# Weight sums of a two-level product moved from accumulating transfers to VectorE additions

## Chip, core and metric

One core of one Trainium2 chip runs the whole kernel. The metric is the device time of one execution in microseconds; the median of three executions is compared. Engines are called TensorE (PE in the rows, PEld its weight loads), VectorE (DVE), ScalarE (ACT), GpSimd (POOL) and SyncE (SP, which only issues transfers).

## The reference, cut to what matters

One decoder layer: a normalised input `h` (1024 prompt tokens and 8 decode tokens, 2048 wide) goes through one wide projection `h @ w_in`, whose columns feed sparse attention with a top-256 indexer, an mLSTM, and gates; the gated outputs go through `w_out` and a final norm.

```python
h = rmsnorm(x, norm_w)
p = split(h @ w_in)                    # q, k, v, indexer, gates, mLSTM q/k/v
att = sparse_attend(p.q, top256(indexer_scores(p.qi, p.ki, p.wi)), p.k, p.v)
ml = mlstm_run(p.mq, p.mk, p.mv, p.ig, p.lf)
x = x + concat(att * silu(p.az), norm(ml) * sigmoid(p.mo) * silu(p.mz)) @ w_out
y = rmsnorm(x, final_norm_w)
```

All of it is float32. The kernel splits each operand of a matmul into a rounded part H and a rest L and sums three products (H H, H L, L H).

## The kernel before, in words

`w_in` is worked through in 61 tiles of 128 columns. Tiles 0 to 20 (misc, indexer queries, attention k, v, q) are plain products in `proj`. Tiles 21 to 60 are the gate stage, `gate_stage`: the tokens are halved, the input rows are halved and the 40 column tiles are taken as 20 pairs (`NP`), so that seven products of half size take the place of eight (a Strassen-like scheme). The seven kinds are called 0 to 7 by the weight operand: kinds 4 to 7 are blocks b11, b12, b21, b22 of the weights as they lie in memory; kinds 1, 2 and 3 are sums of blocks, which have to be made (kind 0, b11 + b12, is only a step on the way to kind 1, which adds b22). Kind 3 is b22 + b12, kind 2 is kind 1 + b21. The order of products is kinds 4 and 6 in turn (20 pairs), then 20 of kind 1, 20 of kind 3, 20 of kind 2, and at last kinds 5 and 7.

The sums are made by transfers. `job_usum` (line 1463) issues for each sum a copy of one block into the DRAM buffer `usD` (from SP, line 1472, or POOL, line 1474) and then, on POOL, a transfer that adds another block to it (`accum_op`, line 1478). A step of the generator is one transfer, a round is four. Within a round, an addition follows the copy that it needs.

`job_usum` and other side work (gates, indexer with top-k search, decode scoring, decode selection `job_dsel`, decode attention, prompt attention, mLSTM) are generators. Three `Lane`s step through their jobs beside the main matmuls: `Lane.step` is called with the time counted in quarter tiles, and each job has a start tile, an end tile and a weight; the steps are spread evenly until the end. Before the change the third lane has "early sums" (64 steps, tile 11.5 to 22) and "late sums" (96 steps, to tile 46). If a product asks for a sum that isn't there, `wget` (line 1708) drives the lane until it is. All engine and transfer queues are in order, and their order is fixed when the kernel is built, by priorities (`tc.high_priority`), ties (`pin`) and a simulated timeline.

A product takes its weights by `wide` (line 1755): a load of 512 KB (or two of 256 KB) into a raw buffer, a cast to H on ScalarE (line 1770) and a subtraction for L on VectorE (line 1771). The ring of raw buffers has one member at first and three from the fourth load on; each member is a pair of 128x512 tiles. Two of the three are loaded whole, the third in two transfers. H and L have three buffers.

Results of a kind are put together with those of the kinds before: `get` (line 1798) loads an intermediate from `spD` into a buffer of the ring `outs`, `combine` (line 1874, its operations are at line 1877) adds PSUM to it on VectorE, `put` (line 1804) stores it. `outs` has four buffers; two more (`ones`, the halves of `rstd`) join it only in the last stage. After the gate stage, `out_weight` (line 1971) splits the first three weight blocks of the output projection; its cast and subtraction are tied into program order.

The lines 1013 and 1035 are the loads of cached indexer keys (`kp`, indirect, on POOL) and their matmuls; 1069 and 1073 are the count and its matmul in `job_dsel`.

Of the kernel before, what the change touches and what calls it, by code (L numbers as in the profile page):

```python
# [8 lines left out]
F32 = mybir.dt.float32  # L9
# [4 lines left out]
OP = mybir.AluOpType  # L14
# [28 lines left out]
T_AK = 9  # L43
T_AV = 11
T_AQ = 13
T_G = 21
# [10 lines left out]
NP = (NT - T_G) // 2  # L57
# [120 lines left out]
def body(tc, A, stop=None):  # L178
    nc = tc.nc
    V, SC, G, PE, SY = nc.vector, nc.scalar, nc.gpsimd, nc.tensor, nc.sync  # L180
# [43 lines left out]
    def paced(name, x):  # L224
        pace[name] = x.ins
        return x

    def dt_(shape, name):
        return tc.dram_tile(shape, F32, name=name)
# [12 lines left out]
    rcS = [dt_([4, S], f"rcS{j}") for j in range(2)]  # L242
    gateS = dt_([2048, R], "gateS")
    xsD = dt_([5, 8, 128, HR], "xsD")
    usD = dt_([4, NP, 128, 2, 4, 128], "usD")
    spD = dt_([3, NP, 128, HR], "spD")
    biasS = [tc.dram_tile([128, (i + 1) * 128], BF16, name=f"biasS{i}") for i in range(8)]

# [801 lines left out]
    def job_dsel():  # L1050
        NP1 = NPG + 1
        with tc.tile_pool(name="dq", bufs=1, side="right") as pd:
# [34 lines left out]
            for bit in (30,) + tuple(range(28, -1, -2)):  # L1087
                n = 1 if bit == 30 else 3
                for y in range(n):
                    v = V.tensor_scalar(cand[:, y], Tt, (y + 1) << bit, None, OP.bitwise_or)  # L1090
                    if not y:
                        pin(v)
                g3 = pd.tile([128, 3, NB, NP1], BF16, name="ri")
                V.tensor_tensor(g3[:, :n], sp.unsqueeze(1).to_broadcast([128, n, NB, NP1]),
                                cand[:, :n].bitcast(F32).unsqueeze(3).to_broadcast([128, n, NB, NP1]), OP.is_ge)
                count(g3[:, :n].rearrange("p y b g -> p (y b) g"), n)
                yield 1400 if n == 1 else 2800
                c = total(n).rearrange("p (y b) -> p y b", y=n)
                yield 300 if n == 1 else 600
                V.tensor_tensor(flag[:, :n], c, kp.unsqueeze(1).to_broadcast([128, n, NB]), OP.is_ge)  # L1100
                for y in range(n):
                    V.copy_predicated(Tt, flag[:, y], cand[:, y])
# [355 lines left out]
                yield 1  # L1458

    sums = set()  # L1460
    NE = 64

    def job_usum():
        def parts(i):
            c1 = T_G + 2 * i - 1
            return [[A["wa"][c, y] for y in range(2)] for c in (c1, c1 + 1)]

        def copy(n, i, src, queue):
            with tc.high_priority():
                if queue is SY:  # L1470
                    with tc.issue_after(pace["dma"]):
                        SY.dma_start(usD[n, i], src)
                else:
                    pin(queue.dma_start(usD[n, i], src))

        def plus(n, i, src):
            with tc.high_priority():
                pin(G.dma_start(usD[n, i], src, accum_op=OP.add, max_dma_last_dim=8192))  # L1478
            sums.add((n, i))

        for i in range(NP + 1):
            (b11, _), (b12, _) = parts(min(i, NP - 1))
            b22 = parts(i - 1)[1][1] if i else None
            if i < NP:
                copy(0, i, b11, SY)
                yield 1
            if i:
                copy(1, i - 1, usD[0, i - 1], G)
                yield 1
            if i < NP:  # L1490
                plus(0, i, b12)
                yield 1
            if i:
                plus(1, i - 1, b22)
                yield 1
        for n, src in ((3, None), (2, 1)):
            for i in range(NP):
                (_, b21), (b12, b22) = parts(i)
                copy(n, i, b22 if n == 3 else usD[1, i], SY if n == 3 else G)
                yield 1  # L1500
                plus(n, i, b12 if n == 3 else b21)
                yield 1

    def att_free():
# [18 lines left out]

    groups = ((2, 3), (4, 5), (6, 7))

    def shares(gen, n):
        g = gen()

        def part(n):
            for _ in range(n):  # L1530
                w = next(g, 0)
                if not w:
                    return
                yield w
        return lambda: part(n), lambda: part(10 ** 6)

    sums_a, sums_b = shares(job_usum, NE)
    lanes = [Lane([Job("gates", 5, T_AK - 0.5, 12500, job_gates),
                   Job("index", T_AK + 1.5, 31.5, 6000 + sum(map(ix_weight, groups)), lambda: job_index(groups)),
                   Job("att", T_G + 17.6, 49.3, 2 * 2 * sum(2 * (1 + (i + 1) * 0.5) for i in range(8)) + 18, job_att, att_free),  # L1540
# [4 lines left out]
                   Job("qrows", T_G + 0.2, 27, 1, job_qrows),  # L1545
                   Job("datt", T_G + 9.2, 38.4, 10000 + 8 * 7000 + 34000 + 5 * 2500 + 8000 + 8000 + 5000, job_datt),
                   Job("dml", T_G + 20, 55.5, 28000 + 16 * 2500 + 5000, job_dml, hi_done)]),
             Lane([Job("early sums", T_AK + 2.5, 22.0, NE, sums_a),
                   Job("late sums", T_AK, 46.0, 8 * NP - NE, sums_b)])]
    gateV = gateS.rearrange("(k p) r -> k p r", p=128)  # L1550
    mixb = [None] * KT
    first = []
# [129 lines left out]
    def gate_stage():  # L1682
# [17 lines left out]
        def take(name, ring):  # L1700
            x = ring[turn[name] % len(ring)]
            turn[name] += 1
            return x
# [2 lines left out]
            return take("ev", outs)  # L1706

        def wget(kind, i):
            if kind < 4:
                while (kind, i) not in sums:  # L1710
                    assert lanes[2]._next() is not None
                return usD[kind, i].rearrange("p q a b -> p q (a b)")
            y, x = divmod(kind - 4, 2)
            return A["wa"][T_G + 2 * i + x - 1, y].rearrange("p q a b -> p q (a b)")
# [40 lines left out]
        def wide(kind, i):  # L1755
            turn["n"] += 1
            if turn["n"] == 4:
                H, L = (wst.plain(name) for name in ("wH", "wL"))
                mlc["bc"] = raws[0][:2]
                raws[:] = [[x[:, 0], x[:, 1], x[:, 0:2]] for x in (H, L)] + [[H[:, 2], L[:, 2], None]]  # L1760
                turn["raw"] = 0
            with tc.high_priority():
                raw = take("raw", raws)
                H, L = (x[turn["w"] % 3] for x in halves)
                turn["w"] += 1
                whole = raw[2] is not None
                for q in (slice(0, 2),) if whole else range(2):
                    r = raw[2] if whole else raw[q]
                    paced("dma", SY.dma_start(r, wget(kind, i)[:, q]))
                    paced("act", SC.copy(H[:, q], r))  # L1770
                    paced("dve", V.tensor_tensor(L[:, q], r, H[:, q].bitcast(F32), OP.subtract))
            return H, L
# [130 lines left out]
                mlc["lo"] = True  # L1903
        del extra, both
        ones += [rstd[:, c * HR:c * HR + HR].rearrange("p (c t) -> p c t", c=2) for c in range(2)]
        turn["p"] = 0

        def two():
            return [take("p", pj), take("p", pj)]
# [29 lines left out]
        def flush():  # L1939
            while muls:  # L1940
                times, ks = muls.pop(0)
                times()
                ready.extend((state["u"], k) for k in ks)
# [27 lines left out]
        def out_weight(q):  # L1971
            H, L, load, cast = wload(A["wo"][0, q], 128, wst, 2, 3)
            pin(load(slice(0, 4)))
            for x in cast(slice(0, 4)):
                pin(x)
            first.append((H, L))

        def last():
# [1 line left out]
            out_weight(2)  # L1980

        flush()
        for p in range(3):
            fetch(p)
        for p, (z, i, y) in enumerate(order):
# [480 lines left out]
```

## Time and profile before

| | us |
|---|---|
| median of three executions (1964.26 to 1969.11) | 1965.51 |
| the profiled execution | 1964.0 |
| its span, first to last instruction | 1962.2 |
| TensorE busy | 1895.3 |
| VectorE busy | 1406.0 |
| ScalarE busy | 914.1 |
| POOL busy | 533.7 |

The profile shows one execution; its mean granted TensorE clock is 0.987 of full speed (2.4 GHz, the other level is 1.2). Busy times of engines overlap. Idle time before an instruction is put down to the wait that ended last; where several waits follow one another (a matmul waits for VectorE, VectorE for ScalarE, ScalarE for a load), the chain has to be followed through the rows of each engine.

### The profile page before, as it was taken

To read this page: it belongs to the slowest core of one execution; us is meant where nothing else is said; L and a number is where in the kernel's file an instruction comes from. 1 tells how busy PE (TensorE), PEld (TensorE's weight loads), DVE (VectorE), ACT (ScalarE), POOL (GpSimd) and SP (SyncE) were. 2 spreads that over 40 slices of the span, in tenths; PEclk is the share of its full clock that TensorE was granted. 3 is DMA by queue.
4 is the path that set the end of the run, shared out by engine and by line. 5 is a ranking of instruction groups with operands and counts; after the bars stand their busy time and mean duration, and the time that the engine had idled before them with its cause. 6 is when DMAs were issued, how large, how long until landed. Compare 5 with 4: busy or idle time off the path is not lost. (4 is left out here: it accounts for less than half of the span.)

```text
span 1962.2 us, 37412 instructions
## 1 busy us (share of the span) xinstructions
PE 1895.3 (97%) x13422; PEld 1820.9 (93%) x13422; DVE 1406.0 (72%) x3261; ACT 914.1 (47%) x1826; POOL 533.7 (27%) x614
## 2 busy tenths in 40 slices
PE   9999998999989999998899999999999989999997
PEld 9999998999979999998799999999999989977776
DVE  8554664767789985897465566657979866787797
ACT  8222252334543557621245565454656634454645
POOL 0599853321100001035111000001211340107632
PEclk9999998999989999999999999999999999999999
DMA  7577767879878759979998874458988778898866
GB/s 258 158 233 217 236 203 223 246 210 228 242 227 246 197 166 270 339 244 266 310 304 239 243 214 143 133 177 294 328 286 294 222 192 269 273 339 300 277 200 220
DMA packets 252918, 474.46 MB, mean 242 GB/s; under 512 B 40549, under 2 KB 116133, under 8 KB 246333
## 3 DMA queue, kind: packets, MB, share of 16 engines
q1 hardware_dynamic: 217261, 356.70, 55.8%
q0 software_dynamic: 21504, 107.32, 21.9%
q10 hardware_dynamic: 13968, 8.06, 1.4%
q8 instruction: 105, 1.72, 0.4%
q14 instruction: 80, 0.66, 0.1%
HBM read 381.54 MB, written 174.32 MB: 283 GB/s over the span
## 5 line engine op out<-in xcount | busy, mean ns | idle before, releaser
L1782 PE MATMUL pj<-xH 128*128 128x258 f32 x1920 | 548.2, 286 | 21.4 <-DVE ev L1877 14.1
L1782 PE MATMUL pj<-xL,xH 128*128 128x258 f32 x1920 | 548.2, 286 | 0.0
L1782 PE MATMUL pj<-xH,xL 128*128 128x258 f32 x1920 | 547.2, 286 | 0.0
L1782 PEld LDWEIGHTS pj<-xH 128*128 128x128 f32 x1920 | 365.2, 190 | 25.3 <-DVE ev L1877 15.3
L1782 PEld LDWEIGHTS pj<-xL,xH 128*128 128x128 f32 x1920 | 365.6, 190 | 2.4 <-issue 0.8
L1782 PEld LDWEIGHTS pj<-xH,xL 128*128 128x128 f32 x1920 | 365.4, 191 | 1.7
L1599 PE MATMUL pj<-xH,wH 128*128 128x344 f32 (+1 forms) x816 | 265.0, 328 | 1.9 <-DVE ev L385 1.1
L1599 PE MATMUL pj<-xL,wH 128*128 128x344 f32 (+1 forms) x816 | 266.2, 326 | 0.0
L1599 PE MATMUL pj<-xH,wL 128*128 128x344 f32 (+1 forms) x816 | 265.4, 326 | 0.0
L263 DVE TENSOR_TENSOR wL<-wraw,wH 128x512 fp32r<-128x512 f32 (+2 forms) x151 | 117.4, 789 | 106.2 <-ACT wH L262 99.9
L1478 POOL DMA_DIRECT2D usD<-in_wa_dram x80 | 66.5, 863 | 428.4 <-DMA usD<-in_wa_dram 228.8
L262 ACT CAST wH<-wraw 128x512 fp32r<-128x512 f32 (+2 forms) x151 | 89.8, 607 | 199.9 <-PE pj L1599 98.3
L1599 PEld LDWEIGHTS pj<-xH,wH 128*128 128x128 f32 x816 | 153.9, 189 | 3.6 <-DVE ev L385 1.8
L1599 PEld LDWEIGHTS pj<-xL,wH 128*128 128x128 f32 x816 | 154.1, 189 | 0.6 <-DVE xL L320 0.3
L1599 PEld LDWEIGHTS pj<-xH,wL 128*128 128x128 f32 x816 | 154.2, 189 | 0.4 <-DVE wL L263 0.3
L1770 ACT CAST xH<-wL 128x1024 fp32r<-128x1024 f32 (+1 forms) x91 | 76.1, 836 | 125.5 <-PE pj L1782 69.8
L1770 ACT CAST xH<-wH 128x1024 fp32r<-128x1024 f32 x91 | 76.0, 836 | 124.4 <-PE pj L1782 72.9
L2153 PE MATMUL pj<-wH,sH 128*128 128x512 f32 x336 | 131.3, 391 | 1.7 <-ACT wH L2137 1.7
L2153 PE MATMUL pj<-wH,sL 128*128 128x512 f32 x336 | 130.7, 390 | 0.0
L2153 PE MATMUL pj<-wL,sH 128*128 128x512 f32 x336 | 125.9, 393 | 4.8 <-DVE wL L2142 4.8
L477 ACT ACTIVATE rl<-bank 128x512 f32<-128x512 f32 (+2 forms) x160 | 79.8, 523 | 99.7 <-PE bank L475 55.1
L480 DVE SCALAR_TENSOR_TENSOR s<-rl,wiN,s 128x512 f32<-128x512 f32 (+2 forms) x150 | 106.6, 729 | 19.5 <-ACT rl L477 16.6
(492 smaller groups left out, 4507.4 us busy)
## 6 DMA issues: line engine op xcount, KB each, us to landing
usD<-in_wa_dram POOLq DMA_DIRECT2D x80, 512.0 KB, 7.8
wraw<-in_wt_dram SPq DMA_DIRECT2D x144, 256.0 KB
usD<-in_wa_dram SPq DMA_DIRECT2D x40, 512.0 KB
usD<-usD POOLq DMA_DIRECT2D x40, 512.0 KB, 7.2
wraw<-in_wa_dram SPq DMA_DIRECT2D x78, 256.0 KB
wraw<-in_wo_dram SPq DMA_DIRECT2D x64, 256.0 KB
ev<-spD SPq DMA_DIRECT2D x62, 258.0 KB
spD<-ev SPq DMA_DIRECT2D x60, 258.0 KB
```

Source lines behind the costliest of these rows:

```text
L262: a = SC.copy(H[:, s, :cols], raw[:, s, :cols])
L263: return a, V.tensor_tensor(L[:, s, :cols], raw[:, s, :cols], H[:, s, :cols].bitcast(F32), OP.subtract)
L477: SC.activation(r[:, :cn], p[:, :cn], AF.Relu)
L480: v = V.scalar_tensor_tensor(s[:, c0:c0 + cn], r[:, :cn], wv, s[:, c0:c0 + cn], OP.mult, OP.add)
L1478: pin(G.dma_start(usD[n, i], src, accum_op=OP.add, max_dma_last_dim=8192))
L1599: m = PE.matmul(ps[:cols, :cn], w_[:, k, :cols], x_[kk][:, c0:c0 + cn], start=(kk == ends[0] and z == 0), stop=(kk == ends[1] and z == 2))
L1770: paced("act", SC.copy(H[:, q], r))
L1782: PE.matmul(ps[c], w_[:, q, ks], x[y][:, c * CS:c * CS + CS], start=(first and q == 0 and k == 0 and z == 0), stop=(q == 1 and k == 3 and ...
L2153: PE.matmul(ps[b], S_[x][:, b * 128:b * 128 + 128], T_[y], start=(k == 0 and z == 0), stop=(k == 7 and z == 2))
```

## The change

Kinds 2 and 3 are no longer made by transfers. `wide` loads both operands of such a sum in halves (kind 2: the sum of kind 1 and b21; kind 3: b22 and b12) into the two tiles of a raw buffer, adds them on VectorE, and casts and subtracts as before; a product of these kinds takes two raw buffers in turn. `usD` has two kinds instead of four, and one job "sums" of 80 steps stands from tile 11.5 to 30.5. In a round, the POOL copy for kind 1 is two rounds behind the SP copy for kind 0, and each addition is one round behind its copy. `job_dsel` issues no step while its lane is between T_G (21) and T_G + 1.2 tiles, and 200 units of its weight move from after the count's matmul to before it. The two buffers of `ones` join `outs` from kind 1 on and leave it before the last stage, to join again at its fifth product as before. The cast and subtraction of `out_weight` are no longer tied, but get priority behind the last weight split.

```diff
-    usD = dt_([4, NP, 128, 2, 4, 128], "usD")
+    usD = dt_([2, NP, 128, 2, 4, 128], "usD")
...
                 count(g3[:, :n].rearrange("p y b g -> p (y b) g"), n)
-                yield 1400 if n == 1 else 2800
+                while T_G <= lanes[1].now / 4 < T_G + 1.2:
+                    yield None
+                yield 1600 if n == 1 else 3200
                 c = total(n).rearrange("p (y b) -> p y b", y=n)
-                yield 300 if n == 1 else 600
+                yield 100 if n == 1 else 200
...
-        for i in range(NP + 1):
-            (b11, _), (b12, _) = parts(min(i, NP - 1))
-            b22 = parts(i - 1)[1][1] if i else None
+        for i in range(NP + 3):
             if i < NP:
-                copy(0, i, b11, SY)
+                copy(0, i, parts(i)[0][0], SY)
                 yield 1
-            if i:
-                copy(1, i - 1, usD[0, i - 1], G)
+            if 2 <= i < NP + 2:
+                copy(1, i - 2, usD[0, i - 2], G)
                 yield 1
-            if i < NP:
-                plus(0, i, b12)
+            if 1 <= i <= NP:
+                plus(0, i - 1, parts(i - 1)[1][0])
                 yield 1
-            if i:
-                plus(1, i - 1, b22)
-                yield 1
-        for n, src in ((3, None), (2, 1)):
-            for i in range(NP):
-                (_, b21), (b12, b22) = parts(i)
-                copy(n, i, b22 if n == 3 else usD[1, i], SY if n == 3 else G)
-                yield 1
-                plus(n, i, b12 if n == 3 else b21)
+            if i >= 3:
+                plus(1, i - 3, parts(i - 3)[1][1])
                 yield 1
...
-             Lane([Job("early sums", T_AK + 2.5, 22.0, NE, sums_a),
-                   Job("late sums", T_AK, 46.0, 8 * NP - NE, sums_b)])]
+             Lane([Job("sums", T_AK + 2.5, 30.5, 4 * NP, job_usum)])]
...
-            if kind < 4:
+            if kind < 2:
                 while (kind, i) not in sums:
...
                 turn["w"] += 1
+                if kind in (2, 3):
+                    pair = (wget(1, i), wget(6, i)) if kind == 2 else (wget(7, i), wget(5, i))
+                    for q in range(2):
+                        raw = raw if not q else take("raw", raws)
+                        for r, src in zip(raw, pair):
+                            paced("dma", SY.dma_start(r, src[:, q]))
+                        V.tensor_tensor(raw[0], raw[0], raw[1], OP.add)
+                        paced("act", SC.copy(H[:, q], raw[0]))
+                        paced("dve", V.tensor_tensor(L[:, q], raw[0], H[:, q].bitcast(F32), OP.subtract))
+                    return H, L
...
         ones += [rstd[:, c * HR:c * HR + HR].rearrange("p (c t) -> p c t", c=2) for c in range(2)]
+        outs += ones
         turn["p"] = 0
+        turn["ev"] = 4
...
             pin(load(slice(0, 4)))
-            for x in cast(slice(0, 4)):
-                pin(x)
+            with tc.high_priority(), tc.issue_after(pace["act"]), tc.issue_after(pace["dve"]):
+                cast(slice(0, 4))
...
         flush()
+        del outs[4:]
         for p in range(3):
             fetch(p)
```

## Rows read from the trace of the kernel before

**Rows 1.** The page, part 1: busy time of each engine, its share of the span, instructions.
```profile
PE 1895.3 (97%) x13422; PEld 1820.9 (93%) x13422; DVE 1406.0 (72%) x3261; ACT 914.1 (47%) x1826; POOL 533.7 (27%) x614
```

**Rows 2.** Stretches: start:end length, busy PE, PEld, DVE, ACT, POOL, granted clock, transfer share, GB/s.
```profile
307.38:314.86 7.48, 0.00 (x1) 0.01 (x1) 0.00 (x0) 0.43 (x1) 3.68 (x5) 0.71 1.04 313
314.86:320.70 5.84, 5.84 (x24) 5.84 (x25) 0.79 (x3) 0.19 (x1) 1.06 (x1) 0.50 1.05 331
531.38:533.61 2.23, 0.00 (x1) 0.03 (x1) 2.23 (x6) 0.45 (x1) 0.03 (x1) 1.00 0.86 314
542.59:547.74 5.15, 0.00 (x1) 0.03 (x1) 4.29 (x19) 2.39 (x5) 1.29 (x2) 0.83 1.01 348
547.74:552.80 5.06, 5.06 (x23) 5.06 (x24) 2.98 (x9) 1.03 (x2) 0.79 (x1) 0.50 1.08 295
553.14:557.13 3.99, 0.00 (x1) 0.01 (x2) 3.95 (x17) 1.03 (x2) 0.52 (x1) 0.89 1.26 353
557.13:563.05 5.92, 5.59 (x26) 5.40 (x26) 5.18 (x21) 2.60 (x5) 0.00 (x0) 0.50 0.07 27
927.24:931.69 4.45, 4.45 (x20) 4.45 (x21) 3.47 (x5) 1.14 (x2) 3.42 (x4) 0.50 0.80 180
945.34:948.76 3.42, 3.42 (x17) 3.42 (x18) 1.06 (x6) 0.79 (x3) 0.34 (x1) 0.50 0.87 346
1608.00:1626.00 18.00, 12.43 (x70) 11.36 (x70) 13.68 (x28) 7.32 (x15) 3.24 (x6) 0.81 0.79 245
```

**Rows 3.** Waits of TensorE, 800 to 990 us: total, times, longest.
```profile
PE pj L1782 <- DVE ev L1877: 14.1, 6, 4.6
```

**Rows 4.** POOL's timeline, 304 to 315 us: start, length, operation, idle time before.
```profile
305.40 0.87 POOL L1478 DMA_DIRECT2D usD<-in_wa_dram  x1 [10.72 <-DMA usD<-usD]
306.57 1.06 POOL L1013 DMA_INDIRECT kp<-in_cik_dram,idx  x1 [0.31 <-issue]
```

**Rows 5.** Timelines of ScalarE and TensorE, start of the gate stage.
```profile
529.71 1.05 ACT L1770 CAST xH<-wraw 128x1024 fp32r<-128x1024 f32 x1 [6.03 <-DMA wraw<-in_wa_dram]
...
557.13 0.20 PE L1073 MATMUL bank<-cb,onesb 128*128 128x24 bf16 x1 [3.99 <-DVE cb L1069]
```

**Rows 6.** A stretch, as in rows 2: 600 to 700 us.
```profile
600.00:700.00 100.00, 100.00 (x750) 95.61 (x749) 90.40 (x187) 46.47 (x80) 5.96 (x8) 1.00 0.75 198
```

**Rows 7.** Waits of SP's queue, 800 to 985 us: total, times, longest.
```profile
SPq L1801 <- DMA spD<-ev: 80.5, 21, 9.1
```

**Rows 8.** Timelines of SP, ScalarE and VectorE, 916 to 927 us.
```profile
916.55 0.37 SPq L1769 DMA_DIRECT2D wL<-usD  x1
...
922.21 1.05 ACT L1770 CAST xH<-wL 128x1024 fp32r<-128x1024 f32 x1 [12.00 <-DMA wL<-usD]
...
926.77 0.42 DVE L1877 TENSOR_TENSOR ev<-pj,ev 128x258 f32<-128x258 f32 x1
```

**Rows 9.** Instructions that write usD, 615 to 1110 us: durations ns, first and last start.
```profile
L1478 POOL DMA_DIRECT2D usD<-in_wa_dram x40: 772/782/1432, 622.8 to 1101.2; - x40
...
L1474 POOL DMA_DIRECT2D usD<-usD x20: 556/758/777, 920.2 to 1092.5; - x20
```

**Rows 10.** Stretches, as in rows 2: the products of kinds 3 and 2.
```profile
920.00:1124.00 204.00, 187.01 (x1459) 180.03 (x1459) 114.97 (x283) 86.21 (x182) 32.31 (x47) 0.97 0.93 275
1124.00:1315.00 191.00, 191.00 (x1535) 187.41 (x1535) 117.81 (x326) 102.76 (x240) 0.00 (x0) 1.00 0.53 159
```

**Rows 11.** Timelines of ScalarE and VectorE, 1600 to 1612 us.
```profile
1604.21 1.12 ACT L262 CAST wH<-wraw 128x512 fp32r<-128x512 f32 x2
...
1608.76 0.69 DVE L263 TENSOR_TENSOR wL<-wraw,wH 128x512 fp32r<-128x512 f32 x1
```

**Rows 12.** Line 2162, an addition on VectorE: durations ns, first and last start, shape.
```profile
L2162 DVE TENSOR_TENSOR yt<-yt,x x21: 677/680/1650, 1871.8 to 1939.6; 128x512 f32<-128x512 f32 x21
```

**Rows 13.** Waits of VectorE, 800 to 990 us: total, times, longest.
```profile
DVE xL L1771 <- ACT xH L1770: 25.9, 12, 7.5
DVE ev L1877 <- DMA ev<-spD: 11.3, 3, 5.7
```

More of the change, by code (lines that the diff above doesn't have):

```diff
@@ L1460, in body, with parts @@
     sums = set()
-    NE = 64
+    def parts(i):
+        c1 = T_G + 2 * i - 1
+        return [[A["wa"][c, y] for y in range(2)] for c in (c1, c1 + 1)]
     def job_usum():
-        def parts(i):
-            c1 = T_G + 2 * i - 1
-            return [[A["wa"][c, y] for y in range(2)] for c in (c1, c1 + 1)]
         def copy(n, i, src, queue):
@@ L1524, in body @@
     groups = ((2, 3), (4, 5), (6, 7))
[L1526 to L1537, printed above, removed]
     lanes = [Lane([Job("gates", 5, T_AK - 0.5, 12500, job_gates),
```

## The prediction

> **What bounds the kernel now.** I read the page first: TensorE is busy for 1895.3 of 1962.2 us [rows 1]. So the kernel ends when TensorE has done its work, and a change that gives TensorE no less to do can only win back time in which it stood idle or ran at half clock. The change doesn't touch the list of matmuls. Next I cut the span into stretches and looked for those where TensorE is not busy all the time; then I asked, for each, which wait ended last. Four places within reach of the edit hold nearly all of it [rows 2, 3].
>
> **A**, at 307 us: TensorE stands 7.48 us, then works 5.84 us at a granted clock of 0.50 [rows 2]. A half clock is worth half its working time, so A costs 7.5 + 2.9 = 10.4 us. **B**, the start of the gate stage: three stalls of 2.23, 5.15 and 3.99 us, and working stretches of 5.06 and 5.92 us at 0.50 [rows 2]. **C**, 800 to 990 us: 14.1 us in six waits of matmuls for VectorE's evacuation [rows 3], and 4.45 and 3.42 us of work at 0.50 (3.9 us lost) [rows 2]: 18.0 us. **D**, the join to the output projection: 18 us hold 12.43 us of TensorE work at a mean clock of 0.81 [rows 2], so 5.6 us idle and at most 0.19 x 18 = 3.4 us of clock: 9.0 us.
>
> **The change part by part.**
>
> *Order of the sums (A).* POOL's queue is in order. An accumulating transfer on it waited 10.72 us for a copy issued just before it, and the indirect load of `kp` stands right behind it, at 306.57 us [rows 4]; TensorE's wait from 307.38 us is for that load. With the copies a round of four steps ahead, an accumulation waits for something older. 80 steps spread over 19 tiles are also thinner than 64 over 10.5 (4.2 a tile against 6.1). Moved past SP's and POOL's queues are all 40 copies (20 on SP, 20 on POOL) and 40 accumulations of the kinds 0 and 1; they are now spread to tile 30.5, where before kind 3 stood, at about the same four steps a tile. I take A as gone whole: 10.4 us. If SP's copy comes late by a round it stays: 0.
>
> *Pause in `job_dsel` (B, third stall).* TensorE waits 3.99 us for the count of the selection, queued on VectorE [rows 5]. For 1.2 tiles from T_G no such step is issued, so this wait and the half clock behind it go: 4.0 + 3.0 = 7.0 us. The steps come later, into stretches where VectorE is at 90.40 of 100 us and TensorE still never idle [rows 6]; there I cost them at nothing, and if that cover fails it is one or two such stalls again, -7 to -14 us.
>
> *First two stalls of B* come from a weight load that ScalarE's cast waited 6.03 us for [rows 5], with VectorE's subtract behind the cast. At that point the ring of raw buffers has one member, and that isn't changed; fewer sums only relieve the transfers. Ends: 0 and 2.2 + 5.15 + 2.5 = 9.9 us. I take 0, since two thirds of the sums' rate stay.
>
> *Six instead of four buffers, and no sums after tile 30.5 (C).* From 800 to 985 us SP waited 80.5 us, 21 times, to load an intermediate into a buffer whose own store had not landed [rows 7]. Weight loads stand behind it: one goes out at 916.55 us, ScalarE's cast, idle 12.00 us, starts at 922.21, VectorE's subtract behind it holds the evacuation until 926.77 [rows 8], and TensorE waits for that. With six buffers the store is two products older. And from 615 to 1101 us 40 accumulations (782 ns each) and 20 copies (758 ns) of half a megabyte leave POOL [rows 9], and 20 copies leave SP; POOL's own time is not on the path, but their traffic is: the transfer engines are at 0.93 from 920 to 1124 us, and at 0.53 once no sums run [rows 10]. I take C as gone: 18.0 us; the lower end is half, if the gathers of the decode attention alone keep the loads late.
>
> *Output weights (D).* ScalarE's casts ran at 1604.21 us, VectorE's subtract only at 1608.76, behind a gate product [rows 11]; the raw buffer and the next load hang on it. Freed of its place in program order it can use VectorE's idle time before. Half of D: 4.5 us (ends 0 and 9.0).
>
> *Additions on VectorE (kinds 3 and 2).* 40 products x 2 halves = 80 additions. The same operation on the same shape takes 680 ns [rows 12]: 54 us of VectorE, inside 395 us in which it is busy for 115 + 118 us [rows 10]. The mean load rises from 59% to 73%, so the work itself is hidden. The casts and subtracts come in halves, which changes only lengths, not the order; SP issues four loads of 256 KB a product instead of one or two. A free engine is the cover; what is not covered is an in-order wait. Each addition waits for two loads, with evacuations and the attention's work queued behind it on VectorE, and TensorE waits for those. The trace has a near relative: the evacuation that waits for its intermediate, one load a product, 60 in three kinds, cost VectorE 11.3 us in three waits [rows 13]. 160 loads make 160/60 x 11.3 = 30 us of VectorE waiting. What of this TensorE feels: between 800 and 990 us VectorE's waits for late data were 25.9 + 11.3 = 37.2 us [rows 13] and TensorE's 14.1 [rows 3], a share of 0.38. So 30 x 0.38 = 11.4 us lost. The ends: 0, if the loads always land in time (the ring of three raw pairs still reaches one and a half products ahead), and 80 x 5.7 x 0.38 = 173 us, if every addition waits like the longest of those three. I take 11.4, as the traffic falls.
>
> **Sum.** 10.4 + 7.0 + 18.0 + 4.5 = 39.9 us won, 11.4 lost, net 28.5. The profiled execution took 1964.0 us (span 1962.2 and 1.8 around it), 1.5 us under the median of the runs, 1965.51. 1964.0 - 28.5 = 1935.5; I forecast 1935.
>
> **Rivals.**
>
> *All of it goes* (the rest of D, the first stalls of B, no new waits): 39.9 + 4.5 + 9.9 = 54.3 us, 1910. For it: TensorE already shows 191 of 191 us from 1124 us on, with the attention beside it [rows 10]. Against: B's first load isn't moved.
>
> *Stalls only change their name.* A keeps its wait on POOL, C is the gathers, and the additions cost what the pause and D bring: 7.0 + 4.5 - 11.4 = 0, so 1964. For it: transfers are at 0.93 in C [rows 10]. Against: the named waits in rows 4 and 7 are on the very transfers that the edit moves.
>
> *Slower: additions block VectorE.* The place is 920 to 1315 us. It decides the sign where an addition waits 1.5 us on average: 80 x 1.5 x 0.38 = 46 us, the gain and the 5.9 us below. At 2.5 us it is 76 us and the time 1964.0 - 39.9 + 76 = 2000. For it: rows 8 show this very mechanism, a subtract waiting for a late load ahead of an evacuation. Against: no matmul of a product waits from 1124 us on [rows 10], and the traffic falls.
>
> *Slower: loads become the bound.* If loads went one pair at a time, each as long as from 916.55 to 922.21 us [rows 8], a product needs 11.4 us where it now has 395/40 = 9.9: 40 x 1.5 = 61 us, 1985. Against: transfers overlap, with 275 GB/s moved from 920 to 1124 us; kinds 3 and 2 need 55 GB/s more than the 159 of the calm stretch [rows 10]. The Trainium skill speaks for this rival (DMA: Bandwidth & Descriptors, section Bandwidth: batch transfers to a megabyte or more; its fit in the section on the anatomy of one DMA is 2.0 us plus the bytes at 436 GB/s): four loads of 256 KB, one after the other, are an estimated 10.4 us against 3.2 for one of 512 KB, which would cost 40 x 0.5 = 20 us here and end at 1944. The rows differ, since they show transfers overlapping.
>
> **How the numbers follow.** Forecast 0.60, all gone 0.17, renamed 0.09, additions block 0.11, loads bound 0.03. A measurement of this kernel can tell about 0.3%, 5.9 us. Faster: 0.60 + 0.17 = 0.77; same 0.09; slower 0.14. The forecast's own range, with A or C halved and additions between 0 and 30 us, is 1915 to 1955. The range that holds 8 in 10 leaves out both slower cases and the far part of "all gone": 1906 to 1968.
>
> **What would show it.** After: no `kp` wait near 307 us; no wait of the selection's matmul just after T_G; SP's waits for `spD` stores down from 80.5 us to a few; no `usD` transfer on POOL after some 800 us; TensorE busy throughout 920 to 1315 us, VectorE near 73% there. Wrong if additions are what VectorE waits for longest and matmuls of L1782 wait for the evacuation in kinds 3 and 2, or if the same four places still stall.

## The result, and the profile after

The changed kernel takes 1978.92 us (median of 7, 1972.02 to 1983.21) against 1964.57 us before on the same chip (median of 7): a ratio of 1.0066, 95% interval 1.0045 to 1.0086. It is slower by 0.66%, where I forecast faster by 1.5%; the measurement is outside the range. The profiled execution of the changed kernel took 1972.02 us, the shortest of its seven, so the trace below can show 8 of the 14 us.

The page of the changed kernel, part 1. TensorE is again busy for most of the span [rows 1]; VectorE has 35 us more to do.

```profile
PE 1899.5 (96%) x13422; PEld 1818.1 (92%) x13422; DVE 1440.9 (73%) x3369; ACT 916.2 (47%) x1854; POOL 489.1 (25%) x554
```

To see where the time went I compared when product n of the gate stage begins (the first matmul of its line) in the two traces, in us; the last columns are worked out from them:

| point | before | after | ahead by |
|---|---|---|---|
| product 0 | 522.48 | 520.32 | 2.2 |
| product 10 | 598.29 | 586.63 | 11.7 |
| product 60 (kind 3 begins) | 919.94 | 914.09 | 5.9 |
| product 80 (kind 2 begins) | 1123.94 | 1092.48 | 31.5 |
| product 110 | 1382.26 | 1388.89 | -6.6 |
| end of the products | 1607.78 | 1614.88 | -7.1 |
| end | 1962.22 | 1970.21 | -8.0 |

The lead at product 80 is the forecast's, but it is no gain yet: part of it is attention work that has moved behind. From product 80 to 110 38 us are lost. The stage from product 60 to 110, as one stretch of either kernel (columns as in rows 2), first before:

```profile
919.94:1382.26 462.32, 444.79 (x3552) 434.02 (x3550) 283.61 (x749) 219.19 (x482) 43.16 (x69) 0.99 0.76 232
```

and after, with the places that answer to A and D in rows 2 and to rows 10:

```profile
291.96:299.17 7.21, 0.00 (x1) 0.00 (x1) 1.52 (x11) 2.82 (x8) 0.00 (x0) 0.76 0.54 132
299.17:302.60 3.43, 3.43 (x14) 3.43 (x15) 0.00 (x0) 0.00 (x0) 0.56 (x1) 0.50 0.36 115
...
1085.00:1315.00 230.00, 215.60 (x1663) 206.39 (x1663) 146.16 (x419) 116.88 (x291) 0.00 (x0) 0.99 0.64 193
914.09:1388.89 474.80, 451.92 (x3555) 434.13 (x3554) 326.07 (x856) 219.02 (x507) 22.57 (x33) 1.00 0.69 218
1615.00:1633.00 18.00, 10.77 (x57) 8.95 (x56) 11.26 (x23) 6.52 (x14) 3.24 (x6) 0.74 0.57 176
```

As many matmuls (3555 and 3552) take 12.5 us longer. Before, TensorE never stopped from 1124 us on [rows 10]; now 14.4 of 230 us from 1085 us on are idle, with the transfers less loaded (218 GB/s against 232). A is still there, only earlier: 7.21 us of waiting instead of 7.48, with 3.43 us of work at half clock behind it instead of 5.84. D holds less work in 18 us than before (10.77 us against 12.43). What TensorE waits for from 1000 to 1310 us (total, times, longest):

```profile
PE bank L694 <- DVE ptL L690: 10.6, 12, 2.0
PE bank L694 <- ACT ptH L689: 2.8, 4, 1.3
PE bank L641 <- DVE qL L625: 1.6, 3, 0.9
```

These are the attention's matmuls, waiting for its low halves `ptL` from VectorE. The matmuls of the products (line 1771) wait for an evacuation for only 2.2 us there. One of the attention's waits, in the timeline (SP, VectorE, TensorE; the bracket is the engine's idle time before, and what ended it):

```profile
1150.16 1.09 SPq L1750 DMA_DIRECT2D wH<-usD  x1
...
1154.17 0.69 DVE L1751 TENSOR_TENSOR wH<-wH 128x512 f32<-128x512 f32 x1 [2.18 <-DMA wH<-usD]
1154.78 0.68 DVE L690 TENSOR_TENSOR ptL<-bank,ptH 128x512 fp32r<-128x512 f32 x1
...
1155.38 0.41 DVE L1866 TENSOR_TENSOR ev<-pj,ev 128x258 f32<-128x258 f32 x1
...
1155.52 0.39 PE L694 MATMUL bank<-ptL,vH 128*128 128x256 f32 x1 [1.94 <-DVE ptL L690]
```

VectorE stands 2.18 us in front of an addition whose load went out 4.0 us before; `ptL` and an evacuation are queued behind it, and TensorE stands 1.94 us for `ptL`. All the additions together (line 1751: durations ns, first and last start; then how long VectorE sat idle before them, us and times):

```profile
L1751 DVE TENSOR_TENSOR wH<-wH x27: 680/692/695, 893.1 to 1264.1; 128x512 f32<-128x512 f32 x27
...
  DMA wH<-usD: 38.5, 24
  DMA wH<-in_wa_dram: 29.3, 15
  DMA wL<-usD: 25.3, 14
  DMA wL<-in_wa_dram: 8.0, 5
  DMA ev<-spD: 1.9, 1
```

That is 103.0 us of waiting in 80 additions, 1.29 us each. The prediction put 30 us there.

### The profile page after: what moved, and what is told of

Read it like the earlier page. It is cut to its first block, busy times and chain, and to the rows that moved or that the text cites. A ratio compares the mean times of both kernels' runs of the same rounds, so it can differ in the third digit from the quotient of the medians.

```text
span 1970.2 us, 37548 instructions
## 1 busy us (share of the span) xinstructions
PE 1899.5 (96%) x13422; PEld 1818.1 (92%) x13422; DVE 1440.9 (73%) x3369; ACT 916.2 (47%) x1854; POOL 489.1 (25%) x554
## 3 DMA queue, kind: packets, MB, share of 16 engines
q0 software_dynamic: 17664, 75.86, 14.4%
## 5 line engine op out<-in xcount | busy, mean ns | idle before, releaser
L1771 PE MATMUL pj<-xH 128*128 128x258 f32 x1920 | 550.2, 287 | 15.7 <-DVE ev L1866 10.5
L1834 POOL DMA_DIRECT2D gateS<-ev x12 | 7.0, 582 | 445.8 <-DVE ev L1833 417.9
L658 ACT ACTIVATE pP<-pP,st 128x512 f32<-128x512 f32 (+3 forms) x96 | 58.2, 607 | 79.0 <-DVE st L653 78.8
L1771 PE MATMUL bank<-xH 128*128 128x258 f32 x320 | 91.0, 284 | 0.5 <-DVE ev L1866 0.5
```

The source lines that it names most:

```text
L658: SC.activation(P[:, :cn], P[:, :cn], AF.Exp, bias=st[:, 2:3], scale=ATT_SCALE, accum_out=st[:, 3 + x:4 + x])
L1771: PE.matmul(ps[c], w_[:, q, ks], x[y][:, c * CS:c * CS + CS], start=(first and q == 0 and k == 0 and z == 0), stop=(q == 1 and k == 3 and ...
```

## The experiments

Each was measured beside the kernel before, whose median was 1962 to 1966 us; ratios are to it, with 95% intervals. Diffs are against the changed kernel. e2, e3, e5, e6, e11, e17 and e18 leave out sums of kinds 2 or 3. The build fixes the order of instructions anew for every kernel, so an edit can also move attention work from beside one product to beside another. I count it by the "other matmuls", those that stand among the matmuls of some products and belong to none of them.

### What of the change costs: e1 to e6

**e1** is the kernel before with the pause, the six buffers and the new `out_weight`; its sums are those of before (two hunks; the rest puts the old job and the old loads back).

```diff
-    usD = dt_([2, NP, 128, 2, 4, 128], "usD")
+    usD = dt_([4, NP, 128, 2, 4, 128], "usD")
...
-             Lane([Job("sums", T_AK + 2.5, 30.5, 4 * NP, job_usum)])]
+             Lane([Job("early sums", T_AK + 2.5, 22.0, NE, sums_a),
+                   Job("late sums", T_AK, 46.0, 8 * NP - NE, sums_b)])]
```

> The kernel before with the pause, the six buffers and the new out_weight; all four sums are made by transfers again, with the order of transfers of before. Theory 1 (the 80 additions hold up VectorE's queue): products 70 to 110 lose their extra 30 us or so, the gate stage keeps what the buffers and the pause give, and the run takes 1935 to 1950 us. Theory 2 (the time lies in attention work moved later by the six buffers and the pause): products 70 to 110 are as long as in the changed kernel and the run takes 1965 to 1980 us. The first kp wait stands at 307 us again either way.

Measured: 1968.2 us, 1.0011 (0.9990 to 1.0032). The time lies in the second theory's range, but not for its reason: products 80 to 110 take 259.0 us, as before (258.3), where the changed kernel takes 296.4. The additions' loss is gone, and so is all that the buffers, the pause and `out_weight` should have won.

**e2** has one load for each half and no addition, **e3** both loads and no addition.

```diff
-                        for r, src in zip(raw, pair):
-                            paced("dma", SY.dma_start(r, src[:, q]))
-                        V.tensor_tensor(raw[0], raw[0], raw[1], OP.add)
+                        paced("dma", SY.dma_start(raw[0], pair[0][:, q]))
```

> The changed kernel without the additions and without the second load of each pair (the sums of kinds 2 and 3 are left out). Theory 1 (VectorE waits inside the queue for the additions' loads): 25 to 30 us are gone from products 70 to 110, 1945 to 1955 us. Theory 2 (moved attention work): within 5 us of the changed kernel, 1970 to 1980 us.

> The changed kernel with both loads of each pair but without the additions (the sums of kinds 2 and 3 are left out). If the in-order wait and the work of the additions on VectorE is the cost, it falls with the additions: 1945 to 1960 us, close to the run with one load. If the loads themselves are the cost, issued late since each half takes a pair of raw buffers, the copies and subtracts wait for them instead: 1970 to 1980 us.

Measured: e2 1949.4 us, 0.9925 (0.9900 to 0.9950); e3 1950.7 us, 0.9927 (0.9902 to 0.9952), both in their first ranges. So the additions cost 1.41% of the kernel, 28 us, and the 80 more loads nothing that can be told. (In e3 nothing reads the second load of a pair: it shows what the traffic costs, not what waiting for that load costs.) The same stretch, products 60 to 110, in e3 (columns as above):

```profile
913.89:1359.57 445.68, 441.65 (x3556) 432.79 (x3554) 288.57 (x778) 223.35 (x509) 13.42 (x25) 0.99 0.72 230
```

It moves more (230 GB/s) than the changed kernel, and is 29 us shorter: the loads are not the bound. The run that leaves out the loads, e2, moves 187 GB/s there and is no shorter:

```profile
910.47:1360.01 449.54, 443.01 (x3555) 433.50 (x3554) 289.51 (x779) 223.77 (x509) 21.25 (x31) 0.99 0.61 187
```

**e5** puts a subtraction of an idle buffer from itself in the addition's place, **e6** an addition of the one load to itself.

```diff
-                        V.tensor_tensor(raw[0], raw[0], raw[1], OP.add)
+                        V.tensor_tensor(raw[1], raw[1], raw[1], OP.subtract)
```

> One load for each half, and in place of the addition a subtraction of the idle raw buffer from itself, which waits for no load of its own product and whose result nobody reads (the sums of kinds 2 and 3 are left out). It measures the additions' bare time on VectorE, 80 of some 0.69 us. If what VectorE spends waiting inside the additions is the cost, this stays near the run with one load: 1948 to 1956 us. If their bare 55 us on VectorE is the cost, most of the 28 us comes back: 1965 to 1980 us.

> One load for each half, and the addition adds that load to itself (the sums of kinds 2 and 3 are left out), so it waits for one load and not for a pair, and the copy waits for the addition. If the cost is the wait for the later load of a pair: 1950 to 1960 us. If it is enough that an addition fed by any load stands in VectorE's queue, or that copy and subtract hang on it: 1965 to 1980 us.

Measured: e5 1945.4 us, 0.9894 (0.9860 to 0.9927), a little under its first range; e6 1957.7 us, 0.9964 (0.9941 to 0.9988), in its first range. e5's VectorE is as loaded as the changed kernel's (321.93 us against 326.07 in this stretch) and the stretch as short as e2's:

```profile
911.21:1361.37 450.16, 440.41 (x3523) 427.84 (x3522) 321.93 (x813) 216.87 (x491) 24.85 (x33) 1.00 0.59 186
```

But e5's subtractions, which wait for nothing, don't stand where the additions stood. All 80 ran before 1024 us, and kind 2 begins at 1035.55 us there; e6's additions run through both kinds (durations ns, first and last start, e5 first):

```profile
L1750 DVE TENSOR_TENSOR wL<-wL x53: 668/683/720, 893.7 to 1023.0; 128x512 f32<-128x512 f32 x53
L1750 DVE TENSOR_TENSOR wH<-wH x53: 674/693/695, 890.5 to 1243.8; 128x512 f32<-128x512 f32 x53
```

And e5's build has the attention elsewhere: 44 other matmuls between products 60 and 80, where e2 has 523. So e5 shows 55 us of bare additions hidden in a stretch with little attention work. What bounds them at their place is e6: bare work and the wait for one load together cost 0.39% (8 us) over e2, with a pair it is 1.41%. So some 20 of the 28 us come with the second load of the pair, and at most 8 are the bare work, as far as e6's own order of instructions allows to tell.

**e4** moves the additions to GpSimd, which has little other work in this stretch (22.57 us: gathers, stores, small operations).

```diff
-                        V.tensor_tensor(raw[0], raw[0], raw[1], OP.add)
+                        G.tensor_tensor(raw[0], raw[0], raw[1], OP.add)
```

> The changed kernel with the additions on GpSimd. If the cost is that the evacuations and subtracts stand behind an addition in VectorE's queue, products 70 to 110 gain 15 to 25 us and the run takes 1950 to 1965 us. If the cost is that the loads come late, nothing is gained: the subtract waits as long, for the same loads, and a slower addition adds to it: 1975 to 1995 us.

Measured: 1972.9 us, 1.0021 (1.0002 to 1.0040), between the two ranges. A third of the 1.4% comes back. The wait is now GpSimd's, and ScalarE's casts, with the attention's casts queued behind them, wait for its additions (waits of e4, 800 to 1320 us: total, times, longest):

```profile
POOL wH L1751 <- DMA wH<-usD: 91.0, 21, 8.4
POOL wH L1751 <- DMA wH<-in_wa_dram: 63.2, 15, 10.1
...
ACT xH L1752 <- POOL wH L1751: 45.5, 19, 4.5
```

and one addition is longer there (line 1751 of e4: durations ns, first and last start):

```profile
L1751 POOL TENSOR_TENSOR wH<-wH x27: 1262/1293/1750, 903.1 to 1294.9; 128x512 f32<-128x512 f32 x27
```

### Which additions, and can the wait be taken away: e17, e18, e7 to e9

**e17** keeps kind 3's additions and second loads alone, **e18** kind 2's (here e17).

```diff
-                        for r, src in zip(raw, pair):
+                        for r, src in zip(raw, pair if kind == 3 else pair[:1]):
                             paced("dma", SY.dma_start(r, src[:, q]))
-                        V.tensor_tensor(raw[0], raw[0], raw[1], OP.add)
+                        if kind == 3:
+                            V.tensor_tensor(raw[0], raw[0], raw[1], OP.add)
```

> The changed kernel with kind 3's additions alone (products 60 to 79); kind 2 has one load and no addition (its sum is left out). With no additions 1949 us, with both 1977 to 1979 us. If additions cost in proportion to their number: 1962 to 1965 us. If only those cost that stand beside the attention's work, which in the changed kernel begins near product 68 and ends near 105: 1952 to 1960 us here, and more than half of the 28 us with kind 2 alone.

> The changed kernel with kind 2's additions alone (products 80 to 99); kind 3 has one load and no addition (its sum is left out). In proportion to their number: 1962 to 1965 us. If the additions cost beside the attention's work, all 20 products of kind 2 stand there: 1965 to 1973 us.

Measured: e17 1947.9 us, 0.9927 (0.9903 to 0.9951), e18 1961.8 us, 0.9994 (0.9975 to 1.0014), both under the ranges that I expected. Kind 3 alone costs nothing, kind 2 alone 0.69% (14 us), and both 1.41%: the two don't add. VectorE's idle time before the additions in e17, and at the end how long ScalarE's cast sat idle for them:

```profile
  DMA wH<-in_wa_dram: 28.9, 13
  DMA wL<-in_wa_dram: 5.9, 5
  DMA ev<-spD: 1.8, 1
...
  ACT xH L1753: 57.3, 19
```

and in e18:

```profile
  DMA wH<-usD: 44.9, 22
  DMA wL<-usD: 19.9, 13
...
  ACT xH L1753: 2.5, 1
```

The last lines bear on a rival: that the loss is not VectorE's queue but the longer chain from load to cast, felt on ScalarE. ScalarE waits 57.3 us in e17, which costs nothing, and 2.5 us in e18, which costs 14 us. So the loss doesn't follow ScalarE's waits.

With kind 3's additions the build has more attention work behind product 80 (304 other matmuls between products 70 and 80 in the changed kernel and 305 in e17, 397 in e2 and in e18). That makes two pairs, with as many matmuls from product 80 to 110 in either kernel of a pair (their order differs in part) and additions in one of them. e2, e18, e17 and the changed kernel (columns as in rows 2):

```profile
1104.03:1360.01 255.98, 255.47 (x2072) 251.47 (x2072) 165.56 (x468) 131.78 (x300) 9.71 (x22) 1.00 0.64 199
1106.25:1377.07 270.82, 261.46 (x2073) 253.90 (x2072) 181.70 (x507) 131.01 (x304) 9.73 (x22) 0.99 0.71 221
1091.71:1365.83 274.12, 274.12 (x2221) 270.13 (x2220) 183.41 (x530) 150.33 (x353) 10.13 (x22) 1.00 0.63 194
1092.48:1388.89 296.41, 282.17 (x2221) 272.89 (x2220) 197.77 (x564) 149.85 (x357) 10.47 (x22) 0.99 0.67 208
```

Kind 2's additions and second loads cost 14.8 us beside e2's attention work and 22.3 us beside that with the moved work. Moving it costs nothing by itself: e17 takes 18 us more than e2 here, and 18 less from product 60 to 80.

**e7** turns the two extra evacuation buffers into a fourth pair of raw buffers; **e8** loads kind 2's transferred sum into the low half's own buffer; **e9** joins them.

```diff
-        outs += ones
...
-        turn["ev"] = 4
...
+        raws.append([rstd[:, x * HR:x * HR + 512] for x in range(2)] + [None])
         for i in range(NP):
             ps = two()
             product(3, i, 0, ps, True, asker(1, i + 2))
...
+        del raws[3:]
         lanes[0].ensure("att")
...
-        del outs[4:]
```

e8:

```diff
                     for q in range(2):
+                        if kind == 2:
+                            low = L[:, q].bitcast(F32)
+                            for r, src in zip((low, raw[q]), pair):
+                                paced("dma", SY.dma_start(r, src[:, q]))
+                            V.tensor_tensor(raw[q], low, raw[q], OP.add)
...
+                            continue
                         raw = raw if not q else take("raw", raws)
```

> The changed kernel with the two added evacuation buffers used as a fourth pair of raw buffers for kinds 3 and 2 instead; evacuations have four buffers as before. If late loads make the additions wait, loads half a product earlier take most of the wait away: 1955 to 1968 us, less what four buffers cost. If the bare additions are the cost, or if the two buffers matter more for the evacuations: 1975 to 1990 us.

> The changed kernel, but kind 2's first source (the transferred sum) is loaded into the low half's own buffer, so that a product of kind 2 takes one pair of raw buffers instead of two and its loads are issued up to a product and a half earlier. If the additions of kind 2 wait for loads that are issued late, their 57 us of waits shrink and 10 to 20 us come back: 1959 to 1970 us. If the cost is the bare addition or has nothing to do with when loads are issued: 1975 to 1982 us.

> The raw ring of four pairs (which gave 0.78% back) and the low half as kind 2's first target (0.48%) together, with four evacuation buffers. If both act by taking waits from the additions: a little under their sum, 1952 to 1962 us, faster than the kernel before by 0.3 to 0.7%. If they remove the same waits: 1960 to 1966 us.

Measured: e7 1963.4 us, 0.9988 (0.9966 to 1.0009); e8 1969.0 us, 1.0018 (0.9997 to 1.0039); e9 1972.5 us, 1.0038 (1.0017 to 1.0058). Against e10 below, which has four evacuation buffers too, the ring is worth 0.28%, not 0.78, and that is no more than the two intervals allow to tell. VectorE's idle time before e7's additions is 80.8 us in all; the largest parts:

```profile
  DMA wH<-usD: 30.5, 19
  DMA wL<-usD: 14.7, 8
  DMA rstd<-usD: 13.9, 8
```

e8's time fell into the range of the late loads, but not for their reason: kind 2's additions still wait

```profile
  DMA xL<-usD: 57.6, 31
```

which is little under the 63.8 us for `usD` in the changed kernel. The loads' own buffers are not the only hold: the longest wait of SP's queue in kind 2 is now 25.1 us, for the attention's results from ScalarE (line 741), and the loads stand in the same queue. And e9 missed: its parts don't add but take back 0.5%, though VectorE waits only 82.7 us inside its additions, near e7's 80.8. Up to product 110 it is 2 us behind e7, and in the output stage 7 us more go, at the casts of output weights and products that the edit doesn't name. I can't say why.

### The other parts: e10 to e12, e14, e16

**e10** is the changed kernel with four evacuation buffers (the three removed lines of e7's diff), **e11** the same edit on e2.

> The changed kernel with four evacuation buffers throughout, as before. The prediction's term C gave the two extra buffers and the missing transfers 18 us together. If the buffers matter: 1985 to 1998 us. If C's stalls went because the transfers of the sums are over by then, and the buffers do nothing: 1974 to 1982 us.

> The run with one load (no additions, no second loads, the sums of kinds 2 and 3 left out) with four evacuation buffers. The same question without the additions: 1949 us again, within 4 us, if the buffers do nothing; 1957 to 1968 us if they carry half or all of the 18 us.

Measured: e10 1969.2 us, 1.0016 (0.9998 to 1.0034); e11 1941.3 us, 0.9868 (0.9843 to 0.9894), both under every range that I gave. The six buffers give nothing; in both pairs they cost half a per cent. With four, the additions cost 1.48% (e10 against e11), as they do with six, and the changed kernel is even with the one before. In C's stretch, 780 to 990 us, e1, with six buffers and transfers, has TensorE wait no less than before [rows 3]:

```profile
PE pj L1784 <- DVE st L1386: 9.1, 1, 9.1
PE pj L1784 <- DVE rstd L1879: 5.0, 2, 2.6
PE pj L1784 <- DVE im L552: 3.6, 1, 3.6
```

whereas in e11, with four buffers and no transfers, its products wait 4.9 us in three waits, though SP's waits for stores, 800 to 985 us, are nearly as long as before [rows 7]:

```profile
SPq L1788 <- DMA spD<-ev: 68.1, 27, 5.2
```

What held C was the transfers and not the wait that SP showed. Whether it was their traffic or their place in POOL's queue, no run tells. What the six buffers cost I haven't found: e2 ends only 2.9 us behind e11 in the profiled runs.

**e12** is the changed kernel without the pause; the hunk of `job_dsel` is undone.

```diff
...
-                while T_G <= lanes[1].now / 4 < T_G + 1.2:
-                    yield None
...
```

> The changed kernel without the pause in the block selection. If the prediction's term B is right the stalls at the start of the gate stage come back and it takes 7 to 10 us more: 1986 to 1990 us. If the products' start is late for another reason: within 3 us of the changed kernel, 1976 to 1982 us.

Measured: 1979.9 us, 1.0065 (1.0041 to 1.0088): no difference at the end. At its place the pause does what I said. Products 0 to 10 take 75.81 us before, 66.31 after, and 72.75 in e12, which has the third stall back (TensorE's waits in e12, products 0 to 10):

```profile
PE bank L1073 <- DVE cb L1069: 4.0, 1, 4.0
```

The changed kernel is 10.5 us ahead of e12 at product 100, and 1.0 at product 110: between the two it has 172 other matmuls to do, e12 94. It was ahead because it had passed over attention work that e12 had done.

**e14** puts the old `out_weight` into e7, **e16** into the changed kernel.

```diff
-            with tc.high_priority(), tc.issue_after(pace["act"]), tc.issue_after(pace["dve"]):
-                cast(slice(0, 4))
+            for x in cast(slice(0, 4)):
+                pin(x)
```

> The kernel with the raw ring of four pairs, with out_weight as before. The prediction's term D gave the new out_weight a gain of 4.5 us: then 1966 to 1969 us. By the stalls at the start of the output stage, which did not shrink, it is worth nothing or a loss: 1957 to 1964 us.

> The changed kernel with out_weight as before, nothing else undone. Term D says the new one gains 4.5 us: then 1982 to 1985 us. If its early casts change the order at the start of the output stage without helping, as the stalls there suggest: 1972 to 1979 us.

Measured: e14 1969.7 us, 1.0028 (1.0017 to 1.0038); e16 1972.4 us, 1.0040 (1.0022 to 1.0058). On e7 the new form gains 0.40%; on the changed kernel it loses 0.26%, where the two intervals overlap. So D's sign isn't settled. In the changed kernel the weight is cast early, and TensorE's waits from 1600 to 1640 us are for the products' own operand:

```profile
PE bank L2078 <- ACT mH L1563: 7.1, 3, 3.2
PE pj L1771 <- DVE ev L1866: 2.7, 1, 2.7
```

### A version that beats both: e13, e15

**e13** is e7 with kind 2's sums made by transfers again, but only between tiles 36 and 46; **e15** is e13 with the old `out_weight`.

```diff
-    usD = dt_([2, NP, 128, 2, 4, 128], "usD")
+    usD = dt_([3, NP, 128, 2, 4, 128], "usD")
...
+        for i in range(NP):
+            copy(2, i, usD[1, i], G)
+            yield 1
+            plus(2, i, parts(i)[0][1])
+            yield 1
...
-             Lane([Job("sums", T_AK + 2.5, 30.5, 4 * NP, job_usum)])]
+             Lane([Job("sums", T_AK + 2.5, 30.5, 4 * NP, sums_a),
+                   Job("late sums", 36.0, 46.0, 2 * NP, sums_b)])]
...
-                if kind in (2, 3):
+                if kind == 3:
```

> The kernel with the raw ring of four pairs (0.9988 of before), with kind 2's sums made by transfers again between tiles 36 and 46; only kind 3's 40 additions are left. Additions cost nothing in products 60 to 70 and all of their time where the attention runs beside them. If it is the attention's chain on VectorE that the additions hold up, kind 2's share, products 80 to 100, comes back: 1946 to 1956 us. If the transfers' traffic costs as much as the additions, as in the run with all transfers: 1960 to 1970 us.

> Both together: raw ring, kind 2 by transfers, out_weight as before. If both parts give what their theories say: 1942 to 1953 us, 0.6% or more under the kernel before. If neither does: 1960 to 1968 us.

Measured: e13 1956.1 us, 0.9955 (0.9941 to 0.9969), at the edge of the first range; e15 1959.7 us, 0.9979 (0.9956 to 1.0001), just under its second. e13 is faster than the kernel before by 0.45%, where the changed kernel is slower than the kernel before by 0.66%. Products 60 to 110:

```profile
916.01:1371.27 455.26, 442.27 (x3533) 430.47 (x3532) 305.70 (x787) 217.22 (x488) 54.51 (x76) 1.00 0.79 248
```

That is 19.5 us less than in the changed kernel, but e13 also has e7's buffers. Against e7 (460.09 us) it is 4.8 us, and 0.33% in the whole: 40 thin late transfers cost a little less than kind 2's 40 additions.

## Why the prediction was wrong

Two things failed: the price of the additions, and the sum of the gains, of which a third came. Either alone would have left the time in the range: with the forecast's gains and the measured price it is 1964.0 - 39.9 + 28 = 1952 us, with the gains of e2 and the forecast's price 1964.0 - 14.7 + 11.4 = 1961 us. Both together turned the sign.

**Additions (forecast 11.4 us, measured 28).** The rival "additions block VectorE" names what happened, at the place it gave: VectorE waits inside additions, matmuls wait for VectorE. Only the matmuls are mainly the attention's, not those of the products that the sign of being wrong named. The step that failed is the scaling "160 loads make 160/60 x 11.3 = 30 us of VectorE waiting": it took the additions' loads to be as punctual as those of an evacuation's intermediate. They waited 103.0 us, 3.4 times as long. The prediction had the reason in hand, a ring that reaches one and a half products ahead, and used it only for the end at 0. A product now takes two of three pairs of raw buffers, and a load often goes out only when an addition has freed its buffer. Waits of SP's queue in the changed kernel, 1060 to 1270 us, for additions to free them:

```profile
SPq L1750 <- DVE wH L1751: 23.5, 12, 4.2
SPq L1750 <- DVE wL L1751: 12.9, 6, 3.3
```

A fourth pair lowered VectorE's waits from 107.4 us (e10) to 80.8 (e7). The rival's deciding wait, 1.5 us an addition, was nearly reached with 1.29. The second factor, 0.38 of VectorE's waiting felt by TensorE, came out at 28/103 = 0.27 as a mean. But it is no constant: 36.6 us of waits cost nothing in e17, 64.8 us cost 14 in e18, and 74.9 us cost 8 in e6. The cover claim, that the work itself is hidden, held for the most part: at most 8 of the 28 us are the bare work (e6).

**A (10.4 us forecast, 1.5 at its place).** The step that failed is "I take A as gone whole": the gather has a path of its own, from its indices to its landing, that holds TensorE about as long. TensorE's wait for `kp` moved to 291.96 us and lasts 7.21; with the half clock behind it, counted as in the prediction, A is 8.9 us now. POOL after (start, length, operation, idle before):

```profile
284.33 1.27 POOL L1013 DMA_INDIRECT kp<-in_cik_dram,idx  x1 [16.99 <-DVE idx L1006]
285.90 0.99 POOL L1013 DMA_INDIRECT kp<-in_cik_dram,idx  x1 [0.30 <-issue]
```

POOL had waited 16.99 us for the gather's indices, so no transfer holds it up there, and TensorE's wait ends 13.3 us after the gather issued at 285.90 us. The lead at the first product is 2.2 us.

**B (7.0 us forecast).** Right at its place: 6.4 us, from e12, which is itself 3.1 us faster there than the kernel before; the first two stalls had been taken as 0. What I left out is what became of the lead: it is gone by product 110, since the attention's work had only been passed over.

**C (18.0 us forecast).** The stalls went: TensorE's waits for evacuations from 780 to 990 us are now 7.8 us, and products 60 to 70 are 23.4 us shorter, about 6 of them moved attention work. Of the two causes that I gave, the transfers are the right one (e11) and the buffers are not (e1, e10): they cost some 10 us. SP's 80.5 us of waits for stores were read as the cause. They were to fall to a few; they are 56.2 us after, with the stalls gone.

**D (4.5 us forecast).** The cast did run earlier, and the wait moved to `mH`; whether the new form gains anything isn't settled (e14, e16).

**The net.** Without additions and transfers the rest of the change is worth 0.75% (e2), 14.7 us of the 39.9 that I summed; without the extra buffers 1.32%, 26 us (e11). 14.7 less 28 for the additions makes the 13 us of loss. The rival "loads become the bound" is refuted by e3 as far as traffic goes. The Trainium skill (DMA: Bandwidth & Descriptors, section Bandwidth) advises transfers of a megabyte or more. By the fit in the Trainium skill (the same page, section Anatomy of one DMA), which is for a transfer issued by GpSimd, the prediction estimated 20 us for four loads of 256 KB one after the other. The runs differ, with 1.3 us between two such loads a product (e2) and four (e3); halves against whole loads no run compares. The range left out the rival whose mechanism rows 8 had already shown.

## What to carry to other kernels

An operation that depends on a load is priced by how early its load goes out, and by what stands behind it in its engine's queue; its own duration may be the smaller part, as it was here. A run that takes the dependence away may also move the operation, so look where it stands before reading the time. Before costing such a wait from a neighbour that takes one load, count the buffers: an operation that halves the look-ahead can make its loads late. A stall gone and a lead at one point are not yet time won while work of lower priority moves behind them: ask at the end of that work, not before.

## What the runs showed of the hardware that was not expected

- Eighty more loads of 256 KB in products 60 to 100 cost nothing, at 230 GB/s against 187 (e3, e2), as long as nothing waited for them.
- Adding 55 us of bare work to VectorE, 290 to 322 us of a 450 us stretch, cost nothing (e5, with the attention moved out of its way), while the same additions with 103 us of waiting for loads cost 28.
- Sums by transfers, which need no addition on VectorE, are not free: e1 is 0.86% over e2 (its early sums and its loads differ too).
- The same addition takes 1293 ns on GpSimd and 692 ns on VectorE.
- Edits that leave the work as it is move the time by up to half a per cent, perhaps through the order of instructions that they give: the new `out_weight` by -0.40% on e7, and by +0.26%, within the intervals, on the changed kernel; e9 is 0.50% over e7. A term of a few us can't be read from one such run.
